# GLA output projection: the first tile pair as plain tiles, its operand sums made behind it

## The chip, the cores and the metric

The kernel runs on one core of a Trainium2 chip. The metric is the device time of one execution in microseconds (us), the median of the runs. Engines: TensorE (PE: matmuls, PEld: weight loads), VectorE (DVE), ScalarE (ACT), GpSimd (POOL), SyncE (SP), and 16 DMA engines that serve the queues of SP and POOL.

## What is computed

One inference step of a two-layer streaming encoder with width 2048, over 512 prompt columns and 64 sample columns (T = 576 in all). Layer 0 mixes by gated linear attention (GLA), layer 1 by a Conformer convolution. The part that matters here is the end of layer 0:

```python
def _gla_mixer(h, w_in, w_a2, b_a, g_norm, w_out, s0):
    proj = h @ w_in
    q, k, v, r, a1 = jnp.split(proj, [...], axis=-1)
    ...
    o, s = _gla_recurrence(qh, kh, vh, ah, s0.astype(f32))      # 4 heads
    o = o * lax.rsqrt(jnp.mean(o * o, axis=-1, keepdims=True) + EPS)
    o = o.reshape(B, L, GLA_DV) * g_norm.astype(f32)
    y = (o.astype(h.dtype) * jax.nn.silu(r)) @ w_out            # the output projection
    return y, s
# layer: x = x + y
```

All of it is in float32, with which the kernel's matmuls deal by splits (below).

## The kernel before

**Splits.** A float32 operand is held as a high part in the format fp32r and a low part, the rest. One product of two operands is three matmuls: high by high, low activation by high weight, high activation by low weight. Activations lie in 16 slots (k = 0 to 15), each of 128 rows and 576 columns, high in `ah[k]`, low in `al[k]`. A matmul takes 288 columns (HT, half of T), so a slot is two matmuls wide. `split` (L697) fills a slot: ScalarE writes the high part, VectorE the low part.

**Weights.** A chunk is 8 weight tiles of 128x128, 512 KB: half of the 16 that one output tile needs. `load_raw` (L114) puts its load on SP's queue. `to_unit` (L120) makes the high part `whi` on ScalarE (L125) and the low part `wlo` either on VectorE (L127) or, for chunks with a source (`src`), as `wlo = -raw` on ScalarE (L129) and an accumulating load of the same weights on POOL's queue (L130). For plain chunks the set `dma_lo` (L624) says which take the second way. `ensure` (L251) prepares chunks in order, `LEAD` = 4 (L282) ahead of the one in use.

**Two ways to a tile pair.** A plain tile takes two chunks of 48 matmuls (`mm_chunk` L272, `run_groups` L295); a pair of plain tiles is 192 matmuls. `run_res` (L474) takes a pair f, f+1 as a 2x2 block product by seven products of 24 matmuls (`prod8` L427, matmul L432), 168 in all: A11, A12 and A22 use quarters of the activations (halves of the slots), and S1 to S4 use sums and differences of those quarters, with sums and differences of weights made on VectorE (`plan_full` L178). The operands of S1 lie in the second halves of the slots 0 to 7, those of S2 to S4 in pages of their own (`sums8`).

**The stage.** The GLA output projection has 16 tiles, 8 pairs, all by `run_res`. Its activations are the gated outputs u = o * silu(r): those of heads 0 to 2 (u0 to u11) are written to DRAM (`spill`, L1047), those of head 3 (u12 to u15) stay in `hd[3]["o"]`. The gate r of head 3 comes out of tile 9, the last group of the input projection, three blocks wide; its PSUM banks are emptied by a Silu on ScalarE (L765, from `rblk` L1037). As there are no free banks, the first products of the output projection take over those of tile 9.

The first pair differs from the other seven. `plan_first` (L213) orders its products A11 A12 A22 S1 S2 S3 S4, and its operands are prepared piece by piece: `early_sums(0)` (called L1178, during head 3's attention) reads head 0's and 2's quarters and makes their sums; behind the release of the attention's pool, `load_first` (L1194) loads two weight halves, `early_sums(1)` (L1195) the next quarters; `first_slots` (L1201), between the halves of tile 9, reads first halves of u0 and u2 and whole u8 and u10, and calls `late_sums` (L1137), which reads u4 and u6 by halves; the rest of the sums follows behind tile 9 (L1211). In all 16 reads of the spill: fourteen of 288 KB and two of 576 KB.

**Order.** The instructions of an engine run in the order that the Tile framework's scheduler gave them, from the program's text, priorities and `issue_after`. An instruction that waits holds up all behind it on its engine; SP's and POOL's loads are issued in the order of their engines.

Of the kernel before, what the change touches and what calls it, by code (L numbers as in the profile page):

```python
# [11 lines left out]
F32 = mybir.dt.float32  # L12
# [37 lines left out]
def emit(nc, tc, x, wg, wa1, wa2, wgo, wc, wco, par, s0, y, sp_out, ss_out, cv_out):  # L50
# [162 lines left out]
    def plan_first(w1, w2, ra):  # L213

        d = {}

        def op(out, a, b, alu=ALU.subtract):
            with tc.high_priority(offset=PRIO):
                nc.vector.tensor_tensor(out, a, b, alu)

        def early():
            d["r1"] = load_raw(w1, 0, "raw1f", *wx[ra])
            d["r3"] = load_raw(w2, 1, "raw3f", *wx["r3"])

        def u0(i):
            to_unit(i, d["r1"], src=w1[:, :8, :])

        def u1(i):
            d["r4"] = load_raw(w1, 1, f"raw{i}")
            to_unit(i, d["r4"], src=w1[:, 8:, :])  # L230

        def u2(i):
            d["r2"] = load_raw(w2, 0, f"raw{i}")
            op(d["r4"], d["r4"], d["r3"])
            op(d["r1"], d["r2"], d["r1"])
            op(d["r4"], d["r4"], d["r1"], ALU.add)
            to_unit(i, d["r4"], src=d["r4"])

        def u4(i):
            op(d["r1"], d["r3"], d["r1"])  # L240
            to_unit(i, d["r1"])

        def u5(i):
            op(d["r2"], d["r3"], d["r2"])
            to_unit(i, d["r2"])

        chunks.extend([u0, u1, u2, lambda i: to_unit(i, d["r1"], src=d["r1"]), u4, u5,
                       lambda i: to_unit(i, d["r3"], src=d["r3"])])
        return early

# [44 lines left out]
    def run_groups(groups, evac, base, between=None):  # L295
        ci = base
        for g in groups:
            pst = [main_tile(f"ps{ci}_{b}") for b in range(len(g))]
            for half in range(2):
                if half and between:  # L300
                    between()
                for bi in range(len(g)):
                    ensure(ci + LEAD)
                    mm_chunk(pst[bi], ci, half)
                    ci += 1
                    if half == 1:
                        evac(g[bi], pst[bi])

# [165 lines left out]
    def run_res(c, f1, f2, addend, evac, first=False, hooks={}):  # L474


        bank2 = lambda n: pool_s[0].tile([P, 512], F32, tag="main", bufs=2, name=f"{n}_{f1}")[:, :HT]
        ps = {n: bank(f"e{n}_{f1}") for n in (("A11", "A12", "A22", "S1") if first else ("A11", "S1", "S3"))}
        ps["S2"] = bank2("es")
        if first:  # L480
            ps["S3"] = bank2("e3")
        ps.setdefault("A12", ps["A11"])
        ps.setdefault("A22", ps["S3"])
        ps["S4"] = ps["S1"]
        sh = wx["sh"].tile([P, HT], F32, tag="sh", bufs=2, name=f"sh{f1}")
        x1, x2 = addend(f1), addend(f2)
        c11, c21, c12, c22 = x1[:, :HT], x1[:, HT:], x2[:, :HT], x2[:, HT:]

        def add(d, n):
            nc.vector.tensor_tensor(d, d, ps[n], ALU.add)  # L490

# [5 lines left out]
        def s3():  # L497
            add(c22, "S3")
            add(c22, "S1")
            if first:  # L500
                add(c21, "S3")
                evac(f1, x1)

        def a22():
            add(c21, "A22")
            if not first:
                evac(f1, x1)

        def a11():
            nc.scalar.activation(sh, ps["A11"], AF.Copy)  # L510
            if first:
                add(c11, "A11")

        def s4():
            add(c12, "S4")
            evac(f2, x2)

        after = {"A11": a11, "A12": lambda: add(c11, "A12"), "A22": a22, "S2": s2, "S3": s3, "S4": s4}
        order = "A11 A12 A22 S1 S2 S3 S4" if first else "A11 S1 S2 S3 A12 A22 S4"
        begun = set()  # L520
        for i, n in enumerate(order.split()):
            ensure(c + i + LEAD)
            prod8(ps[n], n, ready.pop(c + i), ps[n].tensor.name not in begun)
            begun.add(ps[n].tensor.name)
            if n in after:
                after[n]()
            if n in hooks:
                hooks[n]()
# [95 lines left out]
    dma_lo.update(range(4, base_p), range(base_l + 3, base_o), range(base_c + 4, base_co))  # L624
# [138 lines left out]
    def evac_copy(ps, dst, func=AF.Copy):  # L763
        for j in range(2):
            ins = nc.scalar.activation(dst[:, j * HT : (j + 1) * HT], ps[j], func).ins  # L765
        return ins
# [95 lines left out]
    qkp = pool("qkp")  # L862
# [8 lines left out]
    evacs = []  # L871

    def decay(h):
# [4 lines left out]
        c2 = qkp.tile([P, 2, T], F32, tag="qk", name=f"c2_{h}", bufs=3)  # L878
        eq = qkp.tile([P, 2, T], F32, tag="qk", name=f"eq{h}", bufs=3)
# [157 lines left out]
    def rblk(h, vt, ps=None):  # L1037
        if ps is None:
            t = load(blk(h, "r", vt))
        else:  # L1040
            t = tmp(f"r{h}{vt}")
            with tc.high_priority(offset=PRIO):
                evacs.append(evac_copy(ps, t, AF.Silu))
# [33 lines left out]
    def tile(i, ins=None, between=None):  # L1077
# [3 lines left out]
    sums8.update((n, []) for n in ("S2", "S3", "S4"))  # L1081
    S1 = {}
    FIRST, SECOND = slice(0, HT), slice(HT, T)

    def u_pages(h, names=("S3", "S2", "S4")):
        for n in names:
            if (n, h) == ("S4", 3):
                t = [stat.tile([P, 2, HT], F32R, tag="rs", name=f"u{n}_{h}{i}", bufs=2) for i in range(2)]
            else:
                t = (wx["so"] if h else qkp).tile([P, 2, 2, HT], F32R, tag=f"{n}_{h}" if h else "qk", name=f"u{n}_{h}",  # L1090
                                            bufs=1 if h else 3)
                t = (t[:, 0], t[:, 1])
            sums8[n].append(t)

    def u_half(k, hs, t=None):

        if t is None:
            t = tmp(f"u{k}").rearrange("p (k t) -> p k t", k=2)
        nc.sync.dma_start(t, spill[k : k + 2].rearrange("k p t -> p k t")[:, :, hs])
        return t  # L1100

    def put(dst, src):
        nc.scalar.activation(dst[0], src, AF.Copy)
        nc.vector.tensor_tensor(dst[1], src, dst[0].bitcast(F32), ALU.subtract)

    def slots_first(h, a11=None):

        a11 = u_half(2 * h, FIRST) if a11 is None else a11
        for k in range(2 * h, 2 * h + 2):
            ah[k], al[k] = new_slot(k, "u")  # L1110
            put((ah[k][:, :HT], al[k][:, :HT]), a11[:, k % 2, :])

    def slots_s1(h):
        for k in range(2 * h, 2 * h + 2):
            put((ah[k][:, HT:], al[k][:, HT:]), S1[h][:, k % 2, :])

    sub = nc.vector.tensor_tensor

    def early_sums(h):
        u_pages(h)  # L1120
        if h:
            p = [wx["so"].tile([P, 2, 2, HT], F32, tag=n, name=f"u{n}t") for n in ("S4_2", "S2_2")]
            a11, a21, a12, a22 = (t[:, i] for t in p for i in range(2))
        else:
            a11, a21, a12, a22 = (tmp(f"ua{i}").rearrange("p (k t) -> p k t", k=2) for i in range(4))
        for t, k, hs in ((a11, 0, FIRST), (a21, 0, SECOND), (a12, 8, FIRST), (a22, 8, SECOND)):
            u_half(k + 2 * h, hs, t)
        sub(a22, a21, a22, ALU.add)
        sub(a21, a11, a21, ALU.subtract)
        sub(a11, a22, a11, ALU.subtract)  # L1130
        sub(a12, a12, a11, ALU.subtract)
        put(sums8["S3"][h], a21)
        put(sums8["S2"][h], a11)
        put(sums8["S4"][h], a12)
        S1[h] = a22

    def late_sums(h):  # L1137

        if h == 2:
            t = wx["so"].tile([P, 2, 2, HT], F32, tag="S2_3", name="uS2_3t")  # L1140
            a11, a21 = u_half(4, FIRST, t[:, 0]), u_half(4, SECOND, t[:, 1])
        else:
            t = [stat.tile([P, 2, HT], F32, tag="rs", name=f"u6_{i}", bufs=2) for i in range(2)]
            a11, a21 = u_half(6, FIRST, t[0]), u_half(6, SECOND, t[1])
        s3 = tmp(f"s3_{h}").rearrange("p (k t) -> p k t", k=2)
        slots_first(h, a11)
        nc.gpsimd.tensor_tensor(s3, a11, a21, ALU.subtract)

        def rest():
            u_pages(h)  # L1150
            a12, a22 = (u3[:, 2 * h - 4 : 2 * h - 2, hs] for hs in (FIRST, SECOND))
# [389 lines left out]
```

## Time and profile before

| | us |
|---|---|
| median of 3 runs | 1754.13 |
| lowest, highest | 1749.55, 1757.39 |
| the profiled execution | 1755.45 |
| its span, first to last instruction | 1753.8 |

The mean granted TensorE clock of the profiled execution is 0.987 of full speed. Its page gives the busy time of each engine: TensorE 97% of the span, VectorE 67%, ScalarE 53%, POOL 28%. The output projection begins near 721 us of the span and its steady pairs are those from 785 us on. The views used below: the table of stretches (busy time of each engine between two moments), the timeline of one engine (start, length, in brackets the idle time before an instruction and what released it), the chain of waits (from the last instruction back to what released each), and the list of DMA issues with the time to landing. Repeated identical instructions are one row with a count.

### The profile page before, as it was taken

What the parts mean: (1) busy time and instruction counts of PE and PEld (TensorE: products, weight loads), DVE (VectorE), ACT (ScalarE), POOL (GpSimd) and SP (SyncE); (2) the same over time, 40 slices, a digit from 0 to 9 for tenths busy, and PEclk for the clock granted to TensorE, in tenths of its full rate; (3) what the DMA queues carried; (4) which work ended last, traced back from release to release, by engine and by line L of the source; (5) the groups of instructions that cost most, each with busy time, mean ns of one, the idle gap of its engine ahead of it and who ended that gap; (6) DMA issues with size and microseconds to landing.
All of it is one profiled execution on the core that took longest, in us unless ns stands there. A gap on an engine that the chain in (4) does not pass through costs nothing.

```text
span 1753.8 us, 30881 instructions
## 1 busy us (share of the span) xinstructions
PE 1704.2 (97%) x12498; PEld 1679.0 (96%) x12498; DVE 1171.5 (67%) x1650; ACT 925.4 (53%) x1254; POOL 498.2 (28%) x462
## 2 busy tenths in 40 slices
PE   8999999999999999899999999999999999999996
PEld 8999999999999888799999999999999999999995
DVE  7677776767445462878776888878888741285554
ACT  7654434344656674643457555656556574354333
POOL 3100000000123323123223455545555442133221
PEclk9999999999999999999999999999999999999998
DMA  7953555433867866745458777777778778623323
GB/s 242 246 150 116 147 151 151 137 123 123 255 170 230 261 190 184 205 149 172 144 188 199 167 164 164 167 164 164 165 167 175 164 162 169 140 75 124 111 87 134
DMA packets 113920, 289.09 MB, mean 165 GB/s; under 512 B 11088, under 2 KB 41168, under 8 KB 112752
## 3 DMA queue, kind: packets, MB, share of 16 engines
q1 hardware_dynamic: 92368, 208.23, 39.3%
q0 software_dynamic: 21408, 78.88, 22.9%
q8 instruction: 98, 1.61, 0.4%
q14 instruction: 46, 0.38, 0.1%
HBM read 248.05 MB, written 37.45 MB: 163 GB/s over the span
## 4 chain that ended last, share of the span: by engine, by line
PE 85%; DVE 5%; DMA 4%; ACT 2%; issue 1%; POOL 1%; SPq 0%; DVEq 0%; ACTq 0%; POOLq 0%
PE d L432 15%; PE ps L266 14%; PE ps L263 14%; PE ps L269 14%; PE eS L432 5%; PE c L378 4%; PE c L369 3%; PE eA L432 3%; PE db L432 3%; PE pS L1026 2%; PE es L432 1%; PE po L995 1%; DVE c L1376 1%; DMA uS_3t<-spill 1%; DVE x L1437 1%
## 5 line engine op out<-in xcount | busy, mean ns | idle before, releaser
L125 ACT ACTIVATE whi<-raw 128x1024 fp32r<-128x1024 f32 x316 | 334.3, 1060 | 498.0 <-PE ps L266 169.0
L266 PE MATMUL ps<-h1l,whi 128*128 128x288 f32 x1536 | 330.0, 296 | 0.0
L263 PE MATMUL ps<-h1h,whi 128*128 128x288 f32 x1536 | 329.8, 296 | 0.0
L269 PE MATMUL ps<-h1h,wlo 128*128 128x288 f32 x1536 | 329.4, 296 | 0.0
L127 DVE TENSOR_TENSOR wlo<-raw,whi 128x1024 fp32r<-128x1024 f32 x189 | 237.8, 1260 | 128.9 <-ACT whi L125 127.6
L1313 DVE SCALAR_TENSOR_TENSOR acc<-ux,pr,acc 128x606 f32<-128x606 f32 x352 | 297.7, 852 | 11.8 <-ACT acc L1303 2.2
L266 PEld LDWEIGHTS ps<-h1l,whi 128*128 128x128 f32 x1536 | 248.4, 189 | 0.0
L263 PEld LDWEIGHTS ps<-h1h,whi 128*128 128x128 f32 x1536 | 248.1, 189 | 0.0
L269 PEld LDWEIGHTS ps<-h1h,wlo 128*128 128x128 f32 x1536 | 248.0, 189 | 0.0
L1311 POOL TENSOR_TENSOR sd<-sd,sd 128x606 f32<-128x606 f32 x96 | 153.1, 1595 | 71.6 <-ACT sd L1307 70.3
L130 POOL DMA_DIRECT2D wlo<-wc x92 | 80.9, 879 | 216.3 <-ACT wlo L129 163.4
L432 PE MATMUL d<-nh,whi 128*128 128x288 f32 x448 | 132.6, 296 | 0.0
L129 ACT ACTIVATE wlo<-raw 128x1024 fp32r<-128x1024 f32 x127 | 132.5, 1043 | 0.0
L432 PE MATMUL d<-nh,wlo 128*128 128x288 f32 x448 | 131.9, 294 | 0.0
L432 PE MATMUL d<-nl,whi 128*128 128x288 f32 x448 | 131.8, 294 | 0.0
L709 POOL TENSOR_TENSOR ssq<-ssq,sq_x 128x576 f32<-128x576 f32 x35 | 60.0, 1714 | 211.7 <-ACT sq_x L708 205.3
L185 DVE TENSOR_TENSOR raw<-raw,raw 128x1024 f32<-128x1024 f32 x84 | 109.8, 1309 | 10.9 <-DMA raw<-wg 7.4
L1307 ACT ACTIVATE sd<-ux,pr 128x606 f32<-128x606 f32 x112 | 87.3, 793 | 55.6 <-POOL sd L1311 55.6
L263 PE MATMUL ps<-nh,whi 128*128 128x288 f32 x480 | 106.8, 300 | 0.0
L269 PE MATMUL ps<-nh,wlo 128*128 128x288 f32 x480 | 106.5, 300 | 0.0
L266 PE MATMUL ps<-nl,whi 128*128 128x288 f32 x480 | 105.5, 298 | 0.0
L876 POOL DMA_DIRECT2D a<-a3d x4 | 2.5, 617 | 336.8 <-DMA raw<-wg 331.7
(523 smaller groups left out, 3895.2 us busy)
## 6 DMA issues: line engine op xcount, KB each, us to landing
raw<-wc SPq DMA_DIRECT2D x96, 512.0 KB, 5.0
raw<-wg SPq DMA_DIRECT2D x94, 512.0 KB, 4.7
wlo<-wc POOLq DMA_DIRECT2D x92, 512.0 KB, 7.7
wlo<-wg POOLq DMA_DIRECT2D x33, 512.0 KB, 8.4
raw<-wgo SPq DMA_DIRECT2D x30, 512.0 KB, 4.3
raw<-wco SPq DMA_DIRECT2D x26, 512.0 KB, 3.8
ld<-pd SPq DMA_DIRECT2D x29, 288.0 KB, 7.8
vd<-v SPq DMA_DIRECT2D x32, 256.0 KB, 4.6
```

The source lines that it names most:

```text
L125: nc.scalar.activation(hi[:, :w, :], raw, AF.Copy)
L127: nc.vector.tensor_tensor(lo[:, :w, :], raw, hi[:, :w, :].bitcast(F32), ALU.subtract)
L129: nc.scalar.activation(lo, raw, AF.Copy, scale=-1.0)
L130: nc.gpsimd.dma_start(lo, src, accum_op=ALU.add)
L185: nc.vector.tensor_tensor(out, a, b, ALU.subtract)
L263: nc.tensor.matmul(ps[j], hi[:, kk, :], ah[k][:, j * HT : (j + 1) * HT], start=st, stop=False)
L266: nc.tensor.matmul(ps[j], hi[:, kk, :], al[k][:, j * HT : (j + 1) * HT], start=False, stop=False)
L269: nc.tensor.matmul(ps[j], lo[:, kk, :], ah[k][:, j * HT : (j + 1) * HT], start=False, stop=sp)
L432: nc.tensor.matmul(dst, w[:, k, :], v, start=first and k == 0 and i == 0, stop=k == 7 and i == 2, skip_group_check=True)
L1307: nc.scalar.activation(t, u[:, w : w + CW], AF.Copy, scale=cw(w))
L1311: nc.gpsimd.tensor_tensor(side, side, t, ALU.add)
L1313: nc.vector.scalar_tensor_tensor(a, v3(u[:, w : w + CW]), cw(w), a, ALU.mult, ALU.add)
```

## The change

The first pair becomes two plain tiles (`plan([[0, 1]], ...)`, `run_groups([[0, 1]], first_evac, ...)`): four chunks in the order tile 0 first half, tile 1 first half, tile 0 second half, tile 1 second half. The gated outputs of heads 0 to 2 are read once, in six reads of 576 KB, into six pages `pg0` to `pg5` of the pool `so`, which opens when the attention's pool `gp` is released; the former pool `qkp` is part of `gp`. Slots are split from these pages at full width. The sums of heads 0 and 1 are written during tile 9, those of heads 2 and 3 and the S1 halves of the slots (`rest`) behind the plain pair's second chunk; sums are made in place and take over the pages. Pairs 1 to 7 stay as they are, but the two buffers for a pair's first weights alternate the other way round: pair 1 uses the page `ra`, pair 2 the buffer of head 3's outputs. `dma_lo` now holds all four chunks of the plain pair; two subtractions move from POOL to VectorE. `load_raw` loses the condition `hold`, and `run_res` is split into `res_pair`, `steps` and `run_res` with the same products in the same order.

```diff
@@ load_raw
-        with tc.issue_after(state["hold"]) if state.get("hold") else nullcontext():
-            state["dma"] = nc.sync.dma_start(raw, src[:, half * 8 : half * 8 + 8, :])
+        state["dma"] = nc.sync.dma_start(raw, src[:, half * 8 : half * 8 + 8, :])
...
-    def plan_first(w1, w2, ra):
...
@@ run_groups
-    def run_groups(groups, evac, base, between=None):
+    def run_groups(groups, evac, base, between={}):
...
-                if half and between:
-                    between()
                 for bi in range(len(g)):
                     ensure(ci + LEAD)
                     mm_chunk(pst[bi], ci, half)
                     ci += 1
                     if half == 1:
                         evac(g[bi], pst[bi])
+                    if (half, bi) in between:
+                        between[half, bi]()
...
@@ plans
-    load_first = plan_first(wgo[0], wgo[1], "ra")
+    plan([[0, 1]], lambda f: wgo[f])
     for f in range(2, 16, 2):
-        plan_full(wgo[f], wgo[f + 1], ("ra", "rb")[f // 2 % 2])
+        plan_full(wgo[f], wgo[f + 1], ("rb", "ra")[f // 2 % 2])
...
-    dma_lo.update(range(4, base_p), range(base_l + 3, base_o), range(base_c + 4, base_co))
+    dma_lo.update(range(4, base_p), range(base_l + 3, base_o + 4), range(base_c + 4, base_co))
...
@@ heads
-        if h == 3:
-            early_sums(0)
         output(h)
...
     u3 = hd[3]["o"]
-    load_first()
-    early_sums(1)
+    def u_load(k, i):
+        us[k] = so.tile([P, 2, T], F32, tag=f"pg{i}", name=f"u{k}")
+        nc.sync.dma_start(us[k], spill[k : k + 2].rearrange("k p t -> p k t"))
...
+    def u_sums(h, pages):
+        v, w = us[2 * h], us[8 + 2 * h]
+        a11, a12, a21, a22 = v[:, :, :HT], w[:, :, :HT], v[:, :, HT:], w[:, :, HT:]
+        sub = nc.vector.tensor_tensor
+        S1[h], s4 = (a22, a12) if h > 1 else (...)
+        sub(S1[h], a21, a22, ALU.add)
+        sub(a21, a11, a21, ALU.subtract)
+        sub(a11, S1[h], a11, ALU.subtract)
+        sub(s4, a12, a11, ALU.subtract)
+        for (n, src), i in zip((("S2", a11), ("S3", a21), ("S4", s4)), pages):
...
+            put(t, src)
+            sums8[n].append(t)
...
+    for i, k in enumerate((0, 8, 2, 10, 4, 6)):
+        u_load(k, i)
     norm(3)
     gates(3)
...
-    tile(9, turned, first_slots)
...
+    tile(9, turned, {(0, 2): lambda: slots_u(0, 8), (1, 0): lambda: u_sums(0, (8, 9, 10)),
+                     (1, 1): lambda: u_sums(1, (0, 6, 7))})
+    for k in (12, 14):
+        us[k] = u3[:, k - 12 : k - 10, :]
+    slots_u(8, 16)
+
+    def rest():
+        slots_s1(0)
+        slots_s1(1)
+        u_sums(2, (1, 2, 3))
+        slots_s1(2)
+        u_sums(3, (4, None, 5))
+        slots_s1(3)
...
-    for i in range(8):
-        run_res(base_o + 7 * i, 2 * i, 2 * i + 1, go_addend, go_evac, i == 0,
+    def first_evac(f, ps):
+        d = go_addend(f)
+        for j in range(2):
+            js = slice(j * HT, (j + 1) * HT)
+            nc.vector.tensor_tensor(d[:, js], d[:, js], ps[j], ALU.add)
+        go_evac(f, d)
+
+    run_groups([[0, 1]], first_evac, base_o, {(0, 1): rest})
+    for i in range(1, 8):
+        run_res(base_o + 7 * i - 3, 2 * i, 2 * i + 1, go_addend, go_evac,
...
```

SP's queue behind the release of the attention's pool, before (raw140 is the second chunk's weights, raw1f and raw3f the pair's other halves; ld44 is a gate block of head 3; u and uS are reads of the spill; uS2_3 is the read of u4):

```order
L117 DMA raw140_7722<-wgo 128x1024
L117 DMA raw1f_7325<-wgo 128x1024
L117 DMA raw3f_7327<-wgo 128x1024
L1099 DMA uS4_2t_7332<-spill_57 128x2x288 x2
L1099 DMA uS2_2t_7333<-spill_57 128x2x288 x2
L867 DMA ld44_7373<-pd_59 128x576
L1099 DMA u0_7547<-spill_57 128x2x288
L1099 DMA u2_7561<-spill_57 128x2x288
L1207 DMA u8_7575<-spill_57 128x2x576
L1207 DMA u10_7577<-spill_57 128x2x576
L1099 DMA uS2_3t_7579<-spill_57 128x2x288 x2
L1099 DMA u6_0_7592<-spill_57 128x2x288
L1099 DMA u6_1_7593<-spill_57 128x2x288
```

The same place after the change (raw139 to raw141 are the plain pair's second to fourth chunk, raw142, raw143 and raw144 belong to the second pair):

```order
L1094 DMA u0_7301<-spill_57 128x2x576
L1094 DMA u8_7303<-spill_57 128x2x576
L1094 DMA u2_7305<-spill_57 128x2x576
L1094 DMA u10_7307<-spill_57 128x2x576
L1094 DMA u4_7309<-spill_57 128x2x576
L1094 DMA u6_7311<-spill_57 128x2x576
L846 DMA ld44_7338<-pd_59 128x576
L116 DMA raw139_7618<-wgo 128x1024
L116 DMA raw142_7843<-wgo 128x1024
L116 DMA raw144_8001<-wgo 128x1024
L116 DMA raw140_7692<-wgo 128x1024
L116 DMA raw141_7788<-wgo 128x1024
```

Sixteen reads in quarters and halves, spread from head 3's attention to this place and mixed with weights, have become six reads in a row, with one gate block and all further weights behind them.

ScalarE around the first Silu evacuation of tile 9, before (r31 to r33 are the gate blocks that come out of tile 9, uh a slot's high part, uS the high part of a sum):

```order
L1103 ACTIVATE uh4_7583<-uS2_3t_7579 128x288
L1103 ACTIVATE uh5_7587<-uS2_3t_7579 128x288
L125 ACTIVATE whi140_7727<-raw139_7663 128x1024
L129 ACTIVATE wlo140_7728<-raw139_7663 128x1024
L1103 ACTIVATE uh6_7597<-u6_0_7592 128x288
L1103 ACTIVATE uh7_7601<-u6_0_7592 128x288
L1103 ACTIVATE uS4_1_7331<-uS2_2t_7333 128x576
L765 ACT_TABLE_LOAD
L765 ACTIVATE r31_7659<-ps132_0_0_7376 128x288
L765 ACTIVATE r31_7659<-ps132_0_1_7377 128x288
L765 ACTIVATE r32_7718<-ps132_1_0_7378 128x288
L765 ACTIVATE r32_7718<-ps132_1_1_7379 128x288
```

And after:

```order
L680 ACTIVATE uh4_7528<-u4_7309 128x576
L680 ACTIVATE uh5_7532<-u4_7309 128x576
L746 ACT_TABLE_LOAD
L746 ACTIVATE r31_7599<-ps132_0_0_7341 128x288
L746 ACTIVATE r31_7599<-ps132_0_1_7342 128x288
L680 ACTIVATE uh6_7536<-u6_7311 128x576
L680 ACTIVATE uh7_7540<-u6_7311 128x576
L124 ACTIVATE whi139_7620<-raw139_7618 128x1024
L128 ACTIVATE wlo139_7621<-raw139_7618 128x1024
L1097 ACTIVATE uS3_0_7612<-u0_7301 128x576
L1097 ACTIVATE uS2_0_7609<-u0_7301 128x576
L746 ACTIVATE r32_7673<-ps132_1_0_7343 128x288
```

The Silu of the first block stood behind the reads u4 (`uS2_3`) and u6 and a weight chunk; now it stands behind u4 alone, and the second block's Silu behind u6 and a weight chunk.

## Rows read from the trace of the kernel before

**Rows 1.** The page: busy time, share of the span, instructions by engine.

```profile
PE 1704.2 (97%) x12498; PEld 1679.0 (96%) x12498; DVE 1171.5 (67%) x1650; ACT 925.4 (53%) x1254; POOL 498.2 (28%) x462
```

**Rows 2.** Stretches: start:end, length, busy PE, PEld, DVE, ACT, POOL (count), PEclk, DMA share, GB/s.

```profile
676.20:694.50 18.30, 18.30 (x93) 15.41 (x94) 7.07 (x12) 9.31 (x16) 5.43 (x4) 0.91 0.37 87
694.50:721.40 26.90, 26.90 (x202) 26.82 (x202) 19.91 (x30) 14.60 (x22) 2.59 (x3) 1.00 0.94 280
721.40:728.10 6.70, 0.15 (x2) 0.00 (x0) 3.63 (x6) 5.63 (x10) 3.72 (x3) 0.74 0.46 129
728.10:766.30 38.20, 33.65 (x218) 32.21 (x219) 31.31 (x46) 22.84 (x37) 4.05 (x5) 0.91 0.51 137
```

**Rows 3.** TensorE's timeline: start, us, engine, line, op, [idle before <- releaser].

```profile
728.12 0.61 PE L432 MATMUL eA<-uh,whi 128*128 128x288 f32 x1 [6.57 <-ACT r L765]
...
739.85 0.40 PE L432 MATMUL eS<-uh,wlo 128*128 128x288 f32 x1 [0.96 <-DMA wlo<-raw1f]
...
744.00 0.40 PE L432 MATMUL eA<-ul,whi 128*128 128x288 f32 x1 [1.04 <-DVE ul L700]
...
753.97 0.40 PE L432 MATMUL eA<-uh,whi 128*128 128x288 f32 x1 [1.70 <-ACT whi L125]
...
755.23 0.48 PE L432 MATMUL eA<-uh,wlo 128*128 128x288 f32 x1 [0.73 <-DVE wlo L127]
```

**Rows 4.** Chain of waits, steady pairs: start, us, what.

```profile
795.01 3.16 PE eA L432 x24
...
817.32 3.16 PE eA L432 x24
```

**Rows 5.** ScalarE's timeline around the first Silu evacuation.

```profile
722.44 0.78 ACT L1103 ACTIVATE uh<-uS_3t 128x288 fp32r<-128x288 f32 x2 [3.39 <-DMA uS_3t<-spill]
723.12 1.04 ACT L125 ACTIVATE whi<-raw 128x1024 fp32r<-128x1024 f32 x1
...
727.65 1.32 ACT L765 ACTIVATE r<-ps 128x288 f32<-128x288 f32 x4
```

**Rows 6.** Chain of waits, the late read and the second pair's weights.

```profile
709.84 12.57 DMA uS_3t<-spill
...
746.52 6.26 DMA raw<-wgo
```

**Rows 7.** SP's timeline: loads issued behind the pool's release.

```profile
697.25 0.34 SPq L117 DMA_DIRECT2D raw<-wgo  x1
698.00 0.34 SPq L117 DMA_DIRECT2D raw1f<-wgo  x1
```

**Rows 8.** DMA issues, 690 to 735 us: count, KB each, median us to landing.

```profile
raw<-wgo SPq DMA_DIRECT2D x2, 512.0 KB, 4.0
wlo<-wgo POOLq DMA_DIRECT2D x2, 512.0 KB, 8.5
...
raw1f<-wgo SPq DMA_DIRECT2D x1, 512.0 KB, 7.7
```

**Rows 9.** POOL's timeline: an accumulating load.

```profile
734.63 0.88 POOL L130 DMA_DIRECT2D wlo<-raw1f  x1 [6.92 <-ACT wlo L129]
```

**Rows 10.** VectorE's timeline: starts of 576, 288, 1024 columns.

```profile
743.21 0.74 DVE L700 TENSOR_TENSOR ul<-o,uh 128x576 fp32r<-128x576 f32 x1
743.88 0.81 DVE L1104 TENSOR_TENSOR ul<-u,uh 128x288 fp32r<-128x288 f32 x2
744.61 1.21 DVE L127 TENSOR_TENSOR wlo<-raw1f,whi 128x1024 fp32r<-128x1024 f32 x1
745.75 0.74 DVE L1159 TENSOR_TENSOR s<-o,u 128x576 f32<-128x576 f32 x1
```

**Rows 11.** Chain of waits at head 2's spill.

```profile
668.35 7.34 DMA spill<-o
```

**Rows 12.** DMA issues, 655 to 680 us.

```profile
spill<-o SPq DMA_DIRECT2D x4, 288.0 KB, 5.7
```

**Rows 13.** TensorE's timeline behind the spill.

```profile
676.14 0.66 PE L1000 MATMUL pq<-qsm,s 128*128 128x64 f32 x4 [1.67 <-DVE o L1004]
```

More of the change, by code (lines that the diff above doesn't have):

```diff
@@ L211, in plan_full @@
                        lambda i: to_unit(i, d["r3"])])
-    def plan_first(w1, w2, ra):
[L215 to L249, printed above, removed]
     def ensure(n):
@@ L472, in run_full, with res_pair @@
         later.extend([lambda: done(f1, t1), lambda: done(f2, t2)])
[L474 to L484, printed above, removed]
+    def res_pair(f1, f2, addend, evac, ps):
         sh = wx["sh"].tile([P, HT], F32, tag="sh", bufs=2, name=f"sh{f1}")
@@ L487, in run_res, with end, a11, a12 @@
         c11, c21, c12, c22 = x1[:, :HT], x1[:, HT:], x2[:, :HT], x2[:, HT:]
+        left = [2, 2]
         def add(d, n):
             nc.vector.tensor_tensor(d, d, ps[n], ALU.add)
+        def end(n, f, t):
+            left[n] -= 1
+            if not left[n]:
+                evac(f, t)
+        def a11():
+            nc.scalar.activation(sh, ps["A11"], AF.Copy)
+            if ps["A12"] is not ps["A11"]:
+                add(c11, "A11")
+        def a12():
+            add(c11, "A12")
+            end(0, f1, x1)
+        def a22():
+            add(c21, "A22")
+            if ps["A22"] is ps["S3"]:
+                end(0, f1, x1)
         def s2():
@@ L499, in s3, with steps, bank2, run_res @@
             add(c22, "S1")
-            if first:
+            end(1, f2, x2)
+            if ps["A22"] is not ps["S3"]:
                 add(c21, "S3")
[L502 to L512, printed above, removed]
+                end(0, f1, x1)
         def s4():
             add(c12, "S4")
-            evac(f2, x2)
-        after = {"A11": a11, "A12": lambda: add(c11, "A12"), "A22": a22, "S2": s2, "S3": s3, "S4": s4}
-        order = "A11 A12 A22 S1 S2 S3 S4" if first else "A11 S1 S2 S3 A12 A22 S4"
+            end(1, f2, x2)
+        return dict(A11=a11, A12=a12, A22=a22, S1=lambda: None, S2=s2, S3=s3, S4=s4)
+    def steps(c, order):
         begun = set()
-        for i, n in enumerate(order.split()):
+        for i, (n, ps, then) in enumerate(order):
             ensure(c + i + LEAD)
[L523 to L528, printed above, removed]
+            k = ps[n].tensor.name
+            prod8(ps[n], n, ready.pop(c + i), k not in begun)
+            begun.add(k)
+            then()
+    def bank2(name, tag="main"):
+        return pool_s[0].tile([P, 512], F32, tag=tag, bufs=2, name=name)[:, :HT]
+    def run_res(c, f1, f2, addend, evac, hooks={}):
+        ps = {n: bank(f"e{n}_{f1}") for n in ("A11", "S1", "S3")}
+        ps.update(S2=bank2(f"es_{f1}"), A12=ps["A11"], A22=ps["S3"], S4=ps["S1"])
+        then = res_pair(f1, f2, addend, evac, ps)
+        def follow(n):
+            def f():
+                then[n]()
+                if n in hooks:
+                    hooks[n]()
+            return f
+        steps(c, [(n, ps, follow(n)) for n in ("A11", "S1", "S2", "S3", "A12", "A22", "S4")])
     def run_plain(c, f1, f2, addend, evac):
@@ L1042, in rblk @@
             with tc.high_priority(offset=PRIO):
-                evacs.append(evac_copy(ps, t, AF.Silu))
+                evac_copy(ps, t, AF.Silu)
         ob = hd[h]["o"]
@@ L1075, in heads_evac, with tile @@
             nc.sync.dma_start(pd[b][:, j * HT : (j + 1) * HT], t)
-    def tile(i, ins=None, between=None):
+    def tile(i, ins=None, between={}):
         with tc.issue_after(ins) if ins is not None else nullcontext():
             run_groups(gla_last[i : i + 1], heads_evac, base_l + 2 * i, between)
[L1081 to L1151, printed above, removed]
-            s4 = tmp(f"s4_{h}").rearrange("p (k t) -> p k t", k=2)
-            sub(a21, a21, a22, ALU.add)
-            S1[h] = a21
-            slots_s1(h)
-            put(sums8["S3"][h], s3)
-            sub(a11, a21, a11, ALU.subtract)
-            put(sums8["S2"][h], a11)
-            sub(s4, a12, a11, ALU.subtract)
-            put(sums8["S4"][h], s4)
-        return rest
@@ L1198, in emit, with slots_u @@
     rot.update(n=0, heads=False)
-    rests, u2 = [], []
-    def first_slots():
-        for h in range(2):
-            slots_first(h)
-            slots_s1(h)
-        for h in (2, 3):
-            t = so.tile([P, 2, T], F32, tag=f"S3_{h}", name=f"u{2 * h + 4}")
-            nc.sync.dma_start(t, spill[2 * h + 4 : 2 * h + 6].rearrange("k p t -> p k t"))
-            u2.append(t)
-        rests.extend(late_sums(h) for h in (2, 3))
-    tile(9, turned, first_slots)
-    for k in range(8, 12):
-        with tc.issue_after(evacs[1]):
-            split(k, u2[k // 2 - 4][:, k % 2, :], "u")
-    for h in (2, 3):
-        for k in (8 + 2 * h, 9 + 2 * h):
-            with tc.issue_after(evacs[1]):
-                split(k, u3[:, k - 12, :], "u")
-        rests[h - 2]()
+    def slots_u(k0, k1):
+        for k in range(k0, k1):
+            split(k, us[k - k % 2][:, k % 2, :], "u")
+    tile(9, turned, {(0, 2): lambda: slots_u(0, 8), (1, 0): lambda: u_sums(0, (8, 9, 10)),
[10 more added lines that the diff above has]
+        slots_s1(3)
     ssq1 = stat.tile([P, T], F32, tag="ssq", name="ssq1")
```

24 lines of the change are left out of this document (17 added, 7 removed).

## The prediction

> **What bounds the kernel now.** I read the page first. Of the 1753.8 us span TensorE is busy 1704.2 us, 97% [rows 1], so the whole kernel follows TensorE, and a change can pay in two ways only: fewer matmuls, or fewer of the 50 us in which TensorE stands still or runs at a lowered clock. This change adds matmuls, so it must live from the second. The next view is the busy time by stretch around the output projection [rows 2]. The reader is to see that tile 9, the last of the input projection, runs without a hole up to 721.4 us, that the 6.7 us after it hold almost no TensorE work, and that the next 38.2 us, which are the first tile pair and the first two products of the second, are busy for 33.65 us at a mean granted clock of 0.91.
>
> TensorE's own timeline names the holes [rows 3]: 6.57 us before the first product, released by the Silu evacuation `r` of tile 9's banks, then 0.96, 1.04, 1.70 and 0.73 us: 11.0 us together. What an undisturbed stretch looks like is shown by the chain in the pairs behind it [rows 4]: from one A11 product at 795.01 to the next at 817.32 us are 22.31 us for 168 matmuls, or 0.1328 us each. From 721.4 to 766.3 us stand 216 matmuls (168 of the first pair, 24 of A11 and 24 of S1 of the second), which need 28.7 us at that pace and take 44.9. So **16.2 us are lost there**, 11.0 in holes and 5.2 to the lowered clock and slow starts (38.2 us at 0.91 alone are 3.4).
>
> Why the big hole? ScalarE's timeline [rows 5]: it waits 3.39 us for the read `uS_3t`, and behind that conversion, in the fixed order of the engine, stand a weight unit, more conversions and a table load, before the Silu evacuation can run at 727.65 us. The chain says how late that read is: issued at 709.84, landed 12.57 us later at 722.41 us [rows 6]. It is late because it is far back in one queue: SP issues load after load from 697.25 us on [rows 7], and by the order of SP, which stands with the change, this read is the thirteenth of them.
>
> **The change part by part.**
>
> *Matmuls.* The first pair goes from 168 to 192 (4 chunks of 48): +24 x 0.1328 = +3.2 us, all on the path.
>
> *The 16.2 us.* Plain tiles need only the gated outputs themselves, no sums and no sums of weights, so the first chunk needs the slots 0 to 7 and nothing else. Their reads are the first six of the new queue, 576 KB each, 3456 KB. How fast that queue drains I bound from two sides. Slow: before, the thirteen loads (three of 512 KB, two of 576, eight of 288: 4992 KB) were issued from 697.25 us on and had landed by 722.41 us, 198 KB a us [rows 6, 7]. Fast: the stretch moved 280 GB/s in all [rows 2], 273 KB a us if SP's loads had it alone. With the start at 698.0 us, where before the loads into released memory began [rows 7], u6, the sixth, lands at 715.5 (slow) or 710.7 us (fast); it is wanted by k = 6 of the first chunk, at 721.4 + 36 x 0.1328 = 726.2 us. The fifth, u4, behind whose conversion the Silu evacuation of block 0 stands, lands at 712.5 us at the latest. Before, 5.2 us lay between the late landing and the first evacuation, and 1.3 us more until four were done [rows 5, 6]; the same puts the banks free by 719.0 us, before 721.4. The second block's banks are wanted only 6.4 us later. So the 6.57 us go. The 0.96 and 1.04 us also go (no weight sums, no half slots), and so do the 1.70 and 0.73 us: they come from the load of the second pair's first weights, which waited for a buffer and took 6.26 us on the path [rows 6]; after the change that pair uses a page of its own, and the one that takes over the late buffer is the third, whose product is 20 us later. 44.9 us become 240 x 0.1328 = 31.9: **-13.0 us** net of the added matmuls.
>
> *What is late next.* The plain pair's weights of its second to fourth chunk come behind the six reads and one 288 KB load. Each goes raw, then two conversions of 1.0 us on ScalarE [rows 5], then an accumulating load on POOL's queue, 8.5 us to landing [rows 8]. Slow: the second chunk's raw lands at 719.5, its low part at 719.5 + 2.0 + 8.5 = 730.0, wanted at 721.4 + 6.4 + 0.3 = 728.1 us: a wait of 1.9. The third's raw is three 512 KB loads later, 727.3, its low part at 737.8 against 734.2 + 0.3 + 1.9: 1.4 more. The fourth's is in time. Fast: 724.1 against 728.1, no wait. So 0 to 3.3 us; I take **+1.5**, near the middle, since both the slow rate and 8.5 us were read while everything was in flight, and by 721 us the reads are done (the low part of `raw1f`, a copy inside the core, took 5.2 us: issue 734.63, wait ended 739.85 [rows 3, 9]).
>
> *VectorE.* The sums of heads 2 and 3 now follow the plain pair's second chunk. From the last Silu evacuation to the last operand of the second pair's S3 the new order has 13 operations of 576 columns, 10 of 288 and 5 of 1024, at 0.67, 0.37 and 1.14 us from start to start [rows 10]: 18.1 us. That evacuation stands behind the fourth chunk's conversion, 725.5 (fast) to 732.5 us (slow), so the list ends at 743.6 to 750.6. Then come the plain pair's last evacuation, not before 748.4 us, and 4.4 us to the last S2 operand: 755.0 at worst, wanted at 755.7 + 1.5. Cost 0 with 2 us of cover; without it, the second rival's price.
>
> *POOL and the queues.* Two subtractions and one accumulating load leave POOL: no gain, it is 28% busy [rows 1]. On SP the six reads replace sixteen, and four of those sixteen (288 KB each, head 0's) were issued ahead of and between the spill writes of head 2. There one write took 7.34 us [rows 11] where the median was 5.7 [rows 12], and TensorE waited 1.67 us for the buffer that it frees [rows 13], after which 18.3 us ran at a mean clock of 0.91 [rows 2], another 1.65 us. So 0 to -3.3 us: nothing if the write stays as long, all if it takes the median, since then the hole is gone and the clock has no cause to fall. I take **-2.0**.
>
> The dropped issue condition, the list of evacuations and the merged pool move nothing that anyone waits for: at no cost.
>
> Sum: -13.0 + 1.5 - 2.0 = **-13.5 us**. The profiled execution took 1755.45 us (span 1753.8, so 1.65 around it); the median of the three runs is 1754.13, 1.3 lower. I apply the sum to the median: 1740.6 us.
>
> **The rivals.**
>
> 1. *VectorE becomes the bound.* For: in the 38.2 us stretch it was busy 31.31 us, 82%, and not 100% [rows 2]; stretched alike, 18.1 us from 732.5 on become 22.1 and the 4.4 become 5.4, so the last S2 operand comes at 760.0 against 757.2: 2.8 us of wait and 1.65 of clock, -9.1 in all, 1745.0 us. Against: it holds only at the slow queue rate.
>
> 2. *The hole stays* (the change doesn't do what it says). ScalarE's order keeps the Silu evacuation behind a read, u4 now. If u4 landed as late as `uS_3t` did, the hole of 6.57 us would be there again, with 1.65 of clock behind it: -5.3, 1748.8 us. Against: u4 is the fifth load of the queue, not the thirteenth.
>
> 3. *Slower: the two queues share the engines by halves.* All SP loads and POOL's accumulating ones then run at half of 273, 137 KB a us. u6 lands at 723.2, still in time; the second chunk's raw lands at 729.1 and its low part at 739.6, 11.5 us late; the third's is another 4.8 us late. With 3.4 us of lowered clock 19.7 us are lost where 16.2 were, and 3.2 us of matmuls come on top: +6.7, without the spill gain, 1760.8 us. It decides below some 163 KB a us. For: `raw1f` took 7.7 us beside accumulating loads, where a load of its size took 4.0 as a median [rows 8]. Against: 198 KB a us were reached with accumulating loads in flight beside them [rows 6 to 8]. The Trainium skill ("DMA: Bandwidth & Descriptors", section "Queues, rings and completion order") says that an engine takes turns between the queues that have work, a packet at a time; that is this rival's mechanism, and by that rule alone the time would be its 1760.8 us. The trace agrees that loads stretch under it, not that they stretch to half.
>
> **How the numbers follow.** 0.5%, 8.8 us, is about what a measurement of this kernel can tell from no change; the bound for faster is 1745.4 us. The forecast with its bounds (-13.0 + 3.3 = -9.7 to -13.0 - 3.3 = -16.3) is faster throughout: 0.68. The first rival, 0.14, lies on the bound and is split in half. The second, 0.08, is no change. The third, 0.06, is mostly within 0.5%, a third of it beyond. Something unseen, 0.04, is split between no change and slower. Faster 0.75, no change 0.21, slower 0.04. The range runs from 1737 (-16.3, and a little for the scatter of the runs) to 1749, which takes in the first two rivals and leaves out the third and the unseen.
>
> **What would show it.** After the change TensorE's timeline should have no hole of more than 1 us at the start of the plain pair; holes, if any, before its second and third chunk, released by a DMA on `wlo`; the clock at 1.00 over most of the stretch; the second pair's A11 some 25.5 to 29 us after tile 9's end; 24 more matmuls; and at the spill writes of head 2 a smaller hole than 1.67 us. I am wrong on the queue if u4 lands after 716 us or the second chunk's low part after 731; wrong on VectorE if S2 or S3 waits for an operand `uS`; wrong altogether if the plain pair takes over 35 us.

## The result

| | before | after |
|---|---|---|
| median of 7 runs, us | 1757.39 | 1743.68 |
| lowest, highest | 1749.55, 1762.44 | 1737.19, 1745.12 |
| profiled execution, its span | 1755.45, 1753.8 | 1741.84, 1740.1 |

The changed kernel takes 0.9915 of the time, 95% interval 0.9889 to 0.9941: 10 to 20 us less. The forecast was -13.5 us; the medians differ by 13.7, the two profiled executions by 13.6. (Four more runs of before lifted its median from 1754.13, on which the forecast of 1740.6 stood.) Its page begins with the counterpart of [rows 1]: 24 matmuls more, and yet 2.8 us less of busy TensorE.

```profile
PE 1701.4 (98%) x12522; PEld 1677.1 (96%) x12522; DVE 1158.9 (67%) x1641; ACT 924.1 (53%) x1249; POOL 499.2 (29%) x456
```

The stretches of the changed kernel, columns as in [rows 2]: head 3 behind its spill, the rest of tile 9, the plain pair, the second pair's A11 and S1, and from the plain pair to the third pair's A11.

```profile
672.50:690.00 17.50, 17.47 (x96) 14.65 (x97) 1.90 (x5) 8.19 (x13) 5.13 (x4) 1.00 0.37 92
694.50:717.20 22.70, 22.70 (x176) 22.70 (x176) 16.35 (x25) 15.89 (x25) 1.98 (x3) 1.00 0.98 315
717.20:742.70 25.50, 25.12 (x194) 24.90 (x192) 25.50 (x40) 18.44 (x32) 1.72 (x2) 1.00 0.55 134
742.70:751.00 8.30, 7.33 (x55) 7.33 (x56) 8.30 (x13) 5.26 (x8) 2.54 (x1) 1.00 0.43 140
717.20:766.60 49.40, 47.80 (x363) 47.37 (x362) 47.08 (x66) 29.15 (x45) 12.72 (x6) 1.00 0.52 147
```

The 6.7 us without work are gone, the clock is 1.00 throughout, and VectorE is busy 25.50 of 25.50 us beside the plain pair. TensorE's timeline has two holes where [rows 3] had five, 1.61 us instead of 11.0, and at head 3's state product one of 0.70 where [rows 13] had 1.67:

```profile
672.53 0.44 PE L978 MATMUL pq<-qsm,s 128*128 128x64 f32 x2 [0.70 <-DVE o L982]
...
743.67 0.40 PE L393 MATMUL eA<-uh,whi 128*128 128x288 f32 x1 [1.35 <-DVE xr L1171]
...
760.09 0.37 PE L393 MATMUL eS<-uh,whi 128*128 128x288 f32 x1 [0.26 <-DVE xr L443]
```

ScalarE's timeline, against [rows 5]: u4 has landed by 708.27 us, and the first Silu evacuation is done by 711.6, 5.6 us ahead of its use.

```profile
708.27 1.26 ACT L680 ACTIVATE uh<-u 128x576 fp32r<-128x576 f32 x2 [5.83 <-DMA u<-spill]
709.55 1.28 ACT L746 ACT_TABLE_LOAD   x1
710.85 0.71 ACT L746 ACTIVATE r<-ps 128x288 f32<-128x288 f32 x2
```

Where the 13.7 us of span come from, by marks that both traces have:

| from, to | before | after | difference | forecast |
|---|---|---|---|---|
| start, hole at head 3's scores | 635.0 | 633.6 | -1.4 | 0 |
| there, end of tile 9 | 86.4 | 83.6 | -2.8 | -2.0 |
| end of tile 9, third pair's A11 | 60.7 | 49.4 | -11.3 | -13.0 + 1.5 |
| third pair's A11, end | 971.7 | 973.5 | +1.8 | 0 |

(The kernel before weaves two products together at the third pair; its A11 is taken as 12.75 us, four products, ahead of that pair's A12.) The first and last line are scatter: over the twelve profiles of this study the first mark lies anywhere from 629.9 to 637.8 us, and the last projection alone takes 330.0 to 331.7, with no order in it.

### The profile page after: what moved, and what is told of

Same layout as the page of the kernel before. It is cut to its first block, busy times and chain, and to the rows that moved or that the text cites. A ratio compares the mean times of both kernels' runs of the same rounds, so it can differ in the third digit from the quotient of the medians.

```text
span 1740.1 us, 30873 instructions
## 1 busy us (share of the span) xinstructions
PE 1701.4 (98%) x12522; PEld 1677.1 (96%) x12522; DVE 1158.9 (67%) x1641; ACT 924.1 (53%) x1249; POOL 499.2 (29%) x456
## 3 DMA queue, kind: packets, MB, share of 16 engines
q8 instruction: 98, 1.61, 0.4%
## 4 chain that ended last, share of the span: by engine, by line
PE 83%; DVE 7%; DMA 4%; ACT 2%; issue 2%; POOL 1%; SPq 0%; DVEq 0%; ACTq 0%; POOLq 0%
PE d L393 15%; PE ps L230 15%; PE ps L227 15%; PE ps L224 15%; PE c L339 4%; PE eS L393 4%; PE c L330 3%; PE db L393 3%; PE eA L393 2%; PE pS L1004 1%; PE po L973 1%; DVE c L1309 1%; PE es L393 1%; DVE x L1370 1%; DVE wlo L126 1%
## 5 line engine op out<-in xcount | busy, mean ns | idle before, releaser
L690 POOL TENSOR_TENSOR ssq<-ssq,sq_x 128x576 f32<-128x576 f32 x35 | 65.5, 1872 | 215.7 <-ACT sq_x L689 209.0
```

## The experiments

The measure in all of them is the third line of the table, "the distance": from the end of tile 9's last matmul to the third pair's A11. All but one are single profiles, from which holes and distances are read, and no times.

**The scatter.** The changed kernel once more, unaltered.

> The changed kernel once more, unaltered, for the scatter of a single profile: the holes of 1.35 us ahead of the second pair and of 0.70 us at head 3's state product, the 39.0 us between the two holes of head 3 (its scores and its state product), and 49.4 us behind tile 9. If the last two repeat to 0.5 us, single profiles tell differences of 1 us there apart; if not, only larger ones count.

Measured: the distance 49.4 again, the hole ahead of the second pair 1.44 us (1.35), the one before A22 0.22 (0.26). The hole at the state product was not there at all (0.70). So the distance of one and the same program repeats to well under half a microsecond, while head 3 needs several profiles. An edit can also make the scheduler order VectorE's list anew; that happened in two of the runs below, where it is said.

**The Silu evacuations first, in the kernel before.**

```diff
-        slots_first(h, a11)
+        def fill():
+            with tc.issue_after(evacs[1]):
+                slots_first(h, a11)
...
     tile(9, turned, first_slots)
+    for fill in fills:
+        fill()
```

> The kernel before, with one edit: on ScalarE the Silu evacuations of tile 9's first two blocks stand ahead of the conversions of u4 to u7. Measure: from the end of tile 9's last matmul to the start of the third pair's A11 (before 60.9 us, after the change 49.5). Theory (the hole was only the first place where late operands showed; ScalarE, VectorE and the reads behind it cannot follow seven products at TensorE's pace): the 6.57 us hole goes, but holes of about the same sum come back at A12, A22 and the sums, and the measure stays at 58 to 65 us. Rival (the place of the Silu in ScalarE's order was the whole fault): 60.9 - 6.6 - 1.5 = about 52.8 us.

Measured: 64.9 us. The hole is gone, and TensorE goes on with the first product without a pause, but then has eight holes of 13.5 us in sum where there were five of 11.0. The largest, in its timeline:

```profile
724.92 0.40 PE L432 MATMUL eA<-uh,whi 128*128 128x288 f32 x1 [2.36 <-ACT whi L125]
...
739.05 0.40 PE L432 MATMUL eS<-uh,wlo 128*128 128x288 f32 x1 [3.86 <-DMA wlo<-raw1f]
...
755.60 0.40 PE L432 MATMUL eA<-uh,whi 128*128 128x288 f32 x1 [3.91 <-ACT whi L125]
```

All three wait for weights or their low parts. Counted from tile 9's end, S1 gets the low part of its weights after 19.6 us (18.4 before) and the second pair its first weights after 36.1 (32.6 before): what comes behind the closed hole came no earlier, and some of it later. The theory holds; closing one hole gained nothing.

**Seven products, gated outputs read once.**

```diff
-    plan([[0, 1]], lambda f: wgo[f])
+    load_first = plan_first(wgo[0], wgo[1], "ra")
...
-    run_groups([[0, 1]], first_evac, base_o, {(0, 1): rest})
+    steps(base_o, [(n, ps, then[n]) for n in "A11 A12 A22 S1 S2 S3 S4".split()])
```

The lines left out put the first pair's own weight loads behind the six reads and give the second pair the late buffer again.

> The changed kernel with the first pair by seven products again (168 matmuls, order A11 A12 A22 S1 S2 S3 S4, the second pair's first weights in the late buffer as before), but with the six reads of the gated outputs. It separates reading once from the plain tiles. Theory (plain tiles are what pays, as they need no sums for 25 us): VectorE has to make all sums within 10 to 19 us instead of 25 to 35, is not able to, and the measure from tile 9's end to the third pair's A11 is 56 us or more, near the kernel before's 60.9. Rival (early reads are what pays): no holes but the load of the second pair's weights, 28.7 + 15.9 + about 2.4 = 47 us, under the changed kernel's 49.5.

Measured: 65.4 us, in 13 holes, of which TensorE's timeline shows these two as the largest:

```profile
720.58 0.40 PE L431 MATMUL eA<-uh,wlo 128*128 128x288 f32 x1 [2.58 <-DMA wlo<-wgo]
...
755.47 0.61 PE L431 MATMUL eA<-uh,whi 128*128 128x288 f32 x1 [5.48 <-ACT whi L124]
```

The second is the late buffer of the second pair's weights, which this kernel has from before; without its 5.48 us, and some 2.2 more for the 5.43 us behind it at a mean granted clock of 0.60, the distance would still be near 57.7. So reading once is worth nothing by itself here, and the distance is what the theory forecast: **the plain tiles pay**. Its reason is shown only in part: of the other 8.7 us of holes 4.1 wait for accumulating loads of weights, which now stand behind the six reads, 3.6 for VectorE and 1.1 for ScalarE. The plain pair gives VectorE 25 us in which no sum is wanted, and its weights need no sums either. No run has the plain tiles with the sixteen reads, so what they would pay without the single reading is not shown.

**A seventh read ahead of the weights.** One line added behind the six reads.

```diff
+    nc.sync.dma_start(so.tile([P, 2, T], F32, tag="pg8", name="ux"), spill[0:2].rearrange("k p t -> p k t"))
```

> The changed kernel with a seventh read of 576 KB, whose content is not used, between the six reads and the weights on SP's queue: 2.7 us more of queue at 211 KB a us (4256 KB in the 20.2 us from the first issue to the second chunk's raw weights). Theory (the plain pair's low parts come just in time: the second chunk's at 723.1 us against 723.9 wanted): a hole of about 2 us before the second chunk's first matmul with its low part, released by the accumulating load, and nothing of the kind where it is not added. Rival (the queue has several us of cover): no such hole, the measure stays at 49.5 us.

Measured: 49.3 us, and both were half right. A hole is there, but one chunk later than the theory said: the second chunk goes through without one, and the third waits before its first matmul with its low part (the 101st of the pair's 192). TensorE's timeline:

```profile
730.61 0.53 PE L230 MATMUL ps<-uh,wlo 128*128 128x288 f32 x2 [0.88 <-DMA wlo<-wgo]
```

But it costs nothing, because the 1.35 us hole ahead of the second pair is gone. TensorE came 0.9 us later to the bank, and VectorE, whose list this kernel's schedule orders anew, began to empty it 25.2 us behind tile 9's end instead of 26.0; so the run does not show what the lateness alone would have cost. The low parts do come just in time, the third chunk's with the least to spare, but behind them VectorE's list sets the end.

**Low parts of the plain pair on VectorE.** One range is shorter.

```diff
-    dma_lo.update(range(4, base_p), range(base_l + 3, base_o + 4), range(base_c + 4, base_co))
+    dma_lo.update(range(4, base_p), range(base_l + 3, base_o), range(base_c + 4, base_co))
```

> The changed kernel, with the low parts of the plain pair's weights made on VectorE instead of by accumulating loads: four operations of 1.14 us more on VectorE in the stretch in which it is busy 25.5 of 25.5 us. Theory (VectorE sets the end): 3 to 4.6 us of waits come up on TensorE within the second pair, released by VectorE, 52 to 54 us. Rival (VectorE has the 2 us of cover that the prediction gave it, and the accumulating loads were what came just in time): under 51 us.

Measured: 53.3 us, holes of 0.97 and 2.97 us, both released by VectorE. The theory holds.

**The evacuation ahead of head 3's sums.**

```diff
+    def rest3():
+        with tc.issue_after(evd[1]):   # evacuation of the first plain tile
+            u_sums(3, (4, None, 5))
+            slots_s1(3)
...
-    run_groups([[0, 1]], first_evac, base_o, {(0, 1): rest})
+    run_groups([[0, 1]], first_evac, base_o, {(0, 1): rest, (1, 0): rest3})
```

> The changed kernel, with the sums of head 3 made on VectorE behind the evacuation of the first plain tile instead of ahead of it. Measure as before (from tile 9's end to the third pair's A11, 49.4 us after the change). Theory (VectorE's list of sums now sets the end of the stretch, and the 1.35 us hole ahead of the second pair is the evacuation of the plain tile waiting in that list): the hole goes, no operand of S2 or S3 comes late, 48.0 us. Rival (the list has no slack at all): the hole moves to S2 or S3, which then wait 1 to 2 us for an operand uS, and the measure stays at 49 to 50 us.

And in a second kernel besides, for the second pair's first chunk:

```diff
-            to_unit(i, d["r1"])
+            to_unit(i, d["r1"], src=w1[:, :8, :] if lo else None)
```

> As the kernel with the evacuation first, and in addition the low part of the second pair's first weights by an accumulating load instead of on VectorE (1.14 us off VectorE's list, one load more on POOL's queue). Theory: 48 us or a little less, no wait left over 0.3 us in the second pair. Rival (POOL's additions of S2, which the second pair's A22 waits for, are now what comes last): 48 to 49 us with a wait at A22 of 0.5 us or more.

Measured: 50.9 and 48.8 us. In both the hole ahead of the second pair is gone, and the one before A22 has grown from 0.26 us to 1.82 and 1.31. TensorE's timeline of the first kernel has it:

```profile
759.66 0.38 PE L393 MATMUL eS<-uh,whi 128*128 128x288 f32 x1 [1.82 <-DVE xr L443]
```

The stretch behind it ran at a mean granted clock of 0.73, which is why its distance grew by 1.5 us, though its holes came to only 0.2 us more in sum:

```profile
759.60:766.00 6.40, 6.33 (x36) 6.37 (x37) 5.55 (x7) 2.12 (x2) 0.00 (x0) 0.73 0.18 72
```

The first kernel's theory (48.0 us) failed. Its rival was right that the wait moves, but it named the operands of S2 and S3; what is late is the bank of S3, which A22 takes over. The second kernel's rival, which named POOL's additions behind S2, held in both numbers. The bank is free when VectorE has added S3 to c22, and that waits for POOL's three additions behind S2. Two things make these late in the changed kernel. VectorE's list comes to the sum `sh` at 754.78 us, 1.2 us after the last matmul of S2 (753.61); and POOL's timeline shows its additions behind one addition of squares that is booked with 7.70 us.

```profile
748.46 7.70 POOL L690 TENSOR_TENSOR ssq<-ssq,sq_x 128x576 f32<-128x576 f32 x1 [21.33 <-ACT sq_x L689]
756.12 3.33 POOL L467 TENSOR_TENSOR xr<-xr,sh 128x288 f32<-128x288 f32 x3
```

**That addition on VectorE.** One argument more.

```diff
-        add_sq(ssq1, d, f == 0, f"x1{f}")
+        add_sq(ssq1, d, f == 0, f"x1{f}", nc.vector if f == 1 else nc.gpsimd)
```

> The changed kernel, with the addition of the second plain tile's squares on VectorE instead of POOL. It measures the disputed cost by itself. Theory (that one addition lasts 7.7 us on POOL because VectorE runs without a pause beside it): VectorE does it in 0.75 us, POOL's additions behind S2 start within 0.5 us of VectorE's sum sh instead of 0.9 us behind it, themselves still slow (3.3 us for three, 2.3 before the change), and there is no hole before A22. Rival (the 7.7 us are a wait for data that the trace books as busy): the additions start no earlier, and the hole of 0.26 us stays.

Measured: 48.8 us, no hole before A22. VectorE's timeline has the addition with 0.75 us, and then the sum `sh` that POOL waits for:

```profile
750.76 0.75 DVE L690 TENSOR_TENSOR ssq<-ssq,sq_x 128x576 f32<-128x576 f32 x1
...
755.51 0.45 DVE L443 TENSOR_TENSOR sh<-sh,es 128x288 f32<-128x288 f32 x1
```

POOL's has its additions 0.13 us behind the end of `sh` (755.51 + 0.45), where they had been 0.89 behind it (756.12 against 754.78 + 0.45):

```profile
756.09 3.19 POOL L467 TENSOR_TENSOR xr<-xr,sh 128x288 f32<-128x288 f32 x3 [28.92 <-DVE sh L443]
```

The theory holds. The hole ahead of the second pair, which this edit leaves alone, is still there with 0.99 us.

**The evacuation and c22 first.** The edit of the first kernel with the evacuation ahead, and POOL's order in `res_pair`:

```diff
-            for d in (c21, c12, c22):
+            for d in (c22, c21, c12):
                 nc.gpsimd.tensor_tensor(d, d, sh, ALU.add)
```

> The kernel with the evacuation first, and POOL's three additions behind S2 in another order in all pairs: the quarter c22, whose sum with S3 frees the bank that A22 takes over, first instead of last. Theory (the hole before A22 is the bank of S3, freed only behind all three additions, which POOL starts late because its addition of squares runs 6 to 8 us instead of 1.6 beside a dense VectorE): both holes go, 48.0 us from tile 9's end to the third pair's A11 (changed kernel 49.4), and the time is 1 to 2 us below the changed kernel's, which the rounds can hardly tell. Rival (VectorE itself frees the bank late, whatever POOL's order): a hole of 1 us or more stays before A22, 49.5 to 51 us.

Measured: 47.4 us, and no hole from head 3's state product to the end of the projection. The stretch from the plain pair to the third pair's A11:

```profile
714.00:761.40 47.40, 47.40 (x363) 47.36 (x362) 45.12 (x64) 27.98 (x43) 12.71 (x6) 1.00 0.53 153
```

The theory holds. Against the kernel before the ratio is 0.9911 (0.9888 to 0.9935), median 1740.30 us of 6 runs. That is lower than the changed kernel's 1743.68, but the ratios, 0.9911 and 0.9915, are one within their intervals: the 2.0 us that the distance lost are less than the times can tell.

**The early reads put back.** Four lines that issue head 0's reads where the kernel before had them, into scratch.

> The changed kernel with the four 288 KB reads of head 0's and 2's outputs issued again where the kernel before issued them, ahead of and between the spill writes of head 2; what they read is not used. Theory (these reads delayed the last spill write, and TensorE with it): that write lands 7 us or more after its issue, the hole at head 3's state product is 1.5 us or more with a lowered clock behind it, where the changed kernel had 0.70 us and full clock. Rival (the smaller hole was scatter, or came from somewhere else): 0.7 us or less, the write in 6.5 us as after the change. The measure behind tile 9 stays at 49.5 us by both.

Measured: a hole of 0.96 us, between the two, with a clock of 1.00 behind it, and the last write landed 6.47 us after its issue, as in the changed kernel (6.49). This run does not settle it; all twelve profiles together lean towards the theory. In the three kernels with these reads (before, the Silu evacuations first, this one) the last write took 7.34, 7.45 and 6.47 us and the hole was 1.67, 1.95 and 0.96; in the nine without them the write took 5.0 to 6.7, 5.8 in the mean, and the hole was 0 to 1.35. What it is worth in time is less clear: from the scores' hole to tile 9's end the three took 86.4, 84.0 and 84.2 us, the nine 82.5 to 84.2, 83.3 in the mean. That is some 1.6 us for the reads, but 0.8 without the first of the three, whose hole alone had a lowered clock behind it (0.91 over 18.3 us, [rows 2]). Behind the 1.95 us the next 17.3 us ran at 1.00, so the length of the hole does not decide it. The distance of 51.2 us, 1.8 over what both expected, has a hole of 1.59 us before A22 in it, at the place that the runs above explain: this kernel's schedule orders VectorE's list anew, and `sh` begins 38.5 us behind tile 9's end instead of 37.6.

## Why the prediction was right

The mechanism is as forecast, but that the sum fits to 0.2 us is luck: the two lines of scatter in the table alone are -1.4 and +1.8.

*The matmul term and the 16.2 us* (-13.0): as forecast. The plain pair's 192 matmuls and its clock are as worked out, the Silu evacuation, u4 and u6 came early, and the first pair's holes and the late buffer's are gone. One label was wrong: the products that I took for A11 in [rows 4] are A12; the period is the same.

*Low parts late* (+1.5, bounds 0 to 3.3): 0. The queue ran at 211 KB a us (4256 KB from 692.34, the first issue, to 712.5, when ScalarE begins on the second chunk), near the slow bound, but it began 24.9 us ahead of tile 9's end, not 23.4. SP's timeline:

```profile
692.34 3.03 SPq L1094 DMA_DIRECT2D u<-spill  x6
```

POOL issues the accumulating load at 714.89 us:

```profile
714.89 0.86 POOL L129 DMA_DIRECT2D wlo<-wgo  x1 [12.89 <-ACT wlo L128]
```

With 8.2 us to landing, the median of the DMA issues of 690 to 735 us, the low part is there at 723.1; the trace itself dates the landing at 722.73, 1.2 us before the first matmul with it (723.97). The third chunk's had the least to spare: issued at 720.35, landed at 729.38, used at 730.21. The issues:

```profile
u<-spill SPq DMA_DIRECT2D x6, 576.0 KB, 9.5
wlo<-wgo POOLq DMA_DIRECT2D x4, 512.0 KB, 8.2
```

*VectorE* (0, with 2 us of cover): **the step that failed**, by 1.35 us. I followed its list to the last operand of S2 and S3, and these do come in time: the last of S2 was made 33.6 us after tile 9's end (750.04 + 0.75 against 717.2), which is my worst case (755.0 against 721.4), some 1.7 us before its matmul. Two slips stand in that paragraph: the bound of 725.5 us for the start of the list has no working beside it, and the price that it calls the second rival's is the first's. But the same list holds the evacuation of the first plain tile, whose bank the second pair's A11 takes over, and I did not ask when that is wanted: chunk three was done at 736.1 us, the list came to the bank at 743.17, and the product began at 743.67. VectorE's timeline, a sum, the evacuation, and further on the sum `sh` and a low part of weights:

```profile
737.48 0.75 DVE L1109 TENSOR_TENSOR o<-o,u 128x576 f32<-128x576 f32 x1
...
743.17 0.81 DVE L1171 TENSOR_TENSOR xr<-xr,ps 128x288 f32<-128x288 f32 x2
...
754.78 0.45 DVE L443 TENSOR_TENSOR sh<-sh,es 128x288 f32<-128x288 f32 x1
755.15 2.09 DVE L126 TENSOR_TENSOR wlo<-raw,whi 128x1024 fp32r<-128x1024 f32 x1
```

So the first rival's engine was the right one to fear. Its price was put on a wait for sums; the true one was a bank. Two errors, +1.5 and 0 for 0 and +1.35, cancelled by luck.

*POOL* (nothing): 0.26 us before A22, from POOL's long addition, which the prediction did not look for; with that addition on VectorE the 0.26 us are gone.

*Spill* (-2.0, bounds 0 to -3.3): -2.8 between the two profiles, -0.8 to -1.6 over all twelve. The last write and the hole did shrink, as the term has it, but its 1.65 us for the clock rest on one profile: the longer hole above cost no clock.

*The rivals.* The hole did not stay, and the queue did not fall below 163 KB a us: 211 with two accumulating loads beside it. The Trainium skill's rule of turns between queues ("DMA: Bandwidth & Descriptors", "Queues, rings and completion order") therefore did not mean halves here.

## What to carry to other kernels

A trick that saves matmuls but needs prepared operands is dear in the first piece behind a hand-over; the plain form cost 24 matmuls there and bought time to prepare the rest. Closing the largest hole alone, or reading less alone, returned nothing here, since the engines behind it stayed as late as they were. When a list on one engine is followed to its end, ask of every item in it who waits for it, PSUM banks included.

## What the runs showed of the hardware

An elementwise addition on POOL of 128x576 lasted 7.70 us, the same to 0.01 us in five of the profiles (6.73, 6.36 and 5.34 in three others), where its like take 1.57. Beside it VectorE ran one two-input operation after another at their usual lengths; only the last, the one of 2.09 us in the rows above, took longer (1.22 otherwise). The addition ended 1.4 us behind the start of `sh` (754.78 + 1.38 = 756.16), VectorE's first operation in that time with an input from PSUM instead of two from SBUF. It did so in seven of the eight profiles (1.37 to 1.40 us); in the eighth VectorE had paused, from 755.08 to 755.60, and the addition ended at 756.38. This looks as if it stood until then and ran at its own length behind it; no run varies that by itself. Moved to VectorE it took 0.75 us, and POOL's next work began as soon as its data was there. The Trainium skill ("SBUF — State Buffer", section "Who interferes with whom") says that a VectorE `tensor_tensor` with both inputs in SBUF contends with GpSimd's reads of SBUF, and that the shared ports are an exclusive lock; the trace agrees that the two shut each other out, and it shows that POOL's addition waited not for one operation of VectorE but for six more in a row.
